# A streaming encoder layer on one core: the second pair of row tiles in both half-steps by eight products in place of seven

## The chip, the cores and the metric

The program runs on one core of a Trainium2 chip. The metric is the device time of one execution in microseconds (us). The kernel before takes 1363.33 us, the median of 3 runs (1361.89 to 1364.53).

## What is computed

One layer of an encoder for 592 tokens: 16 meta tokens, 512 of a prompt and 64 of a running stream, with model width 1024. It has five parts in a row, with residual adds:

```python
x = x + 0.5 * swiglu(rmsnorm(x, g1), ffn1_w1, ffn1_w3, ffn1_w2)
p = rmsnorm(x, g2) @ w_in
x = x + concat(rwkv(p), mla(p)) @ w_out
x = x + 0.5 * swiglu(rmsnorm(x, g3), ffn2_w1, ffn2_w3, ffn2_w2)
y = rmsnorm(x, g4)

def swiglu(h, w1, w3, w2):
    return (silu(h @ w1) * (h @ w3)) @ w2
```

The first and the fourth part are the two half-steps that the change touches. Their inner width is 2816, that is 22 row tiles of 128. The middle holds a recurrent mixer (8 heads, chunks of 64 tokens) and an attention (8 heads). Inputs and outputs are f32.

## The kernel before

**Number format.** A wide product is made of split operands: each weight and each activation is a high part, cast by ScalarE (ACT), and a low part, which is the remainder and is made by a subtraction (line 130) on VectorE (DVE) or GpSimd (POOL). One f32 product is then three matmuls, high by high, high by low, low by high (lines 153 to 155 in `mm3`, 323 to 325 in `product`).

**A half-step** (`ffn`, tag f1 or f2). Tokens are cut into two halves of 296 columns (288 in f2). The row tiles go in 11 pairs, row tile p with row tile p + 11, and each row tile stands for a tile of w1 (j = 0) and one of w3 (j = 1). For one j, a pair is a two-by-two block product: two row tiles by two halves of the 1024 inputs (index kh), times two halves of the inputs by two halves of the tokens. It can be done in two ways:

- `plain`: eight block products, 24 matmuls of one token half for each output tile, 192 for a pair. The operands are the four plain blocks "11", "21", "12", "22" (the input x times its gain, split). The norm's factor is applied when an output tile leaves PSUM (line 357, `scaled`), so the matmuls need no finished norm.
- `pair`: seven block products, 168 matmuls for a pair. It needs sums of weight blocks (lines 405 to 408, POOL, 1024 wide), their split parts, and four combined operand blocks "t1" to "t4", which need the norm of both token halves.

Pair 0 is done by `plain`, pairs 1 to 10 by `pair`. After them come the second products (`down`, outputs f1o and f2o, added into x at line 441); the first `down` needs pairs 0 and 1, and stands behind pair 2 in the program.

**Operands.** `Operands` makes the plain blocks (lines 258 and 259), the norm (squares added at line 169, line 176 sums, line 179 the reciprocal, line 183 spreads it) and, in `combined`, the blocks t1 to t4 in four steps: four products of x with gain and norm (line 277, DVE), four differences (line 279), four splits. ON_POOL says which of these go to POOL: in f1 the fourth difference and the splits of t1, t2 and t3, in f2 the split of t3. For pair 1 it also sends low parts of weight sums to POOL: s3 in f1, all four of s1 to s4 in f2.

**Order.** The string START[tag] interleaves the first steps: "a" and "b" step the operands of the two token halves, "t" the combined blocks, "0" and "1" the generators of pairs 0 and 1. The framework then places each instruction by a timeline of its own, on priorities that follow the order of writing. Each engine runs its queue strictly in the order that comes out; this holds for the middle of the program too. Weight blocks live in 7 buffers (raw2), their split parts in 4 + 4 (rings hi, lo, hi2, lo2), outputs in 8 PSUM banks. All transfers are issued from one queue, SP's.

In the middle, POOL solves 62 steps for each of 8 units of the mixer (lines 788 and 790). The result goes out to memory (line 792, qd), comes back (line 796, qt) and is transposed on DVE (line 803).

Of the kernel before, what the change touches and what calls it, by code (L numbers as in the profile page):

```python
# [45 lines left out]
ATTENTION = ((10, 0, 5), (11, 0, 4), (13, 0, 5), (13, 0, 7), (15, 0, 4), (12, 0, 7), (8, 0, 1), (11, 1, 13))  # L46


START = {"f1": "0aaaaaaa0aaa0babbbbbb0bbbb000tt00tt11", "f2": "aa0aaaaaba0ba1bb0babb0babb00b00tttt0"}
ON_POOL = {"n1": ("4", "t1", "t2", "t3"), "n1_0": ("sums",), "n1_1": (), "f1": ("s3",), "n2": ("t3",), "n2_0": (),  # L50
           "n2_1": (), "f2": ("s3", "s2", "s4", "s1")}
LOADS = ((0, (0,)), (0, (2,)), (0, (4,)), (0, (6,)), (0, ()), (1, (0, 2, 4, 6)))
AHEAD = 2
# [27 lines left out]
def build(ctx: ExitStack, tc: tile.TileContext, I, O):  # L81
# [64 lines left out]
    def mm3(outs, ws, xs, ks):  # L146

        n = len(ks)
        for out, w in zip(outs, ws):
            for i, k in enumerate(ks):  # L150
                xh, xl = xs(k)
                wh, wl = w[k]
                T.matmul(out, wh, xh, start=i == 0, stop=False)  # L153
                T.matmul(out, wh, xl, start=False, stop=False)  # L154
                T.matmul(out, wl, xh, start=False, stop=i == n - 1)  # L155
# [142 lines left out]
    def ffn(tag, x, ops, w13, w2, gp, n0, n1, between=iter(())):  # L298
# [9 lines left out]
        def parts(t, nm, sub=V):  # L308

            out = []  # L310
            for j, (pool, sfx) in enumerate(((ring, ""), (gp, "2"))):
                hi, lo = (pool.tile([128, 4, 128], F32R, tag=q + sfx, bufs=4, name=f"{nm}_{q[0]}{j}")
                          for q in ("hi", "lo"))
                split(hi, lo, t[:, j], sub)
                out.append((hi, lo))
            return out

        def product(nm, w, b):
            bh, bl = ops.get(b)
            for j, (wh, wl) in enumerate(w):  # L320
                out = fbank(f"{nm}{j}")[:, :n]
                for k in range(4):
                    T.matmul(out, wh[:, k], bh[k], start=k == 0, stop=False)  # L323
                    T.matmul(out, wh[:, k], bl[k], start=False, stop=False)
                    T.matmul(out, wl[:, k], bh[k], start=False, stop=k == 3)  # L325
                yield j, out

        def blocks(nm, p):
            A = {}
            for i, kh in ((0, 0), (0, 1), (1, 0), (1, 1)):  # L330
                A[i, kh] = gp.tile([128, 2, 4, 128], F32, tag="raw2", bufs=7, name=f"{nm}A{i}{kh}")
                src = w13[p + HM * i][:, :, 4 * kh:4 * kh + 4]
                if p == 0 and i == 0:
                    for j in range(2):
                        next(between, None)
                        nc.sync.dma_start(A[i, kh][:, j], src[:, j])
                else:
                    next(between, None)
                    nc.sync.dma_start(A[i, kh], src)
            return A  # L340

        def scratch(nm, tag, bufs=2):
            return [gp.tile([128, 296], F32, tag=tag, bufs=bufs, name=f"{nm}{j}")[:, :n] for j in range(2)]

        def gate(nm, p, i, h, h1, h3):
            si = tmp.tile([128, 320], F32, tag="sq", name=f"{nm}si{i}{h}")[:, :n]
            S.activation(si, h1, AF.Silu)
            if p == HM - 1 and (i, h) == (1, 0):
                load_sqrt(eps[:, 0:1])
            V.tensor_tensor(si, si, h3, ALU.mult)  # L350
            gh, gl = (gp.tile([128, 296], F32R, tag=q, bufs=12, name=f"{nm}{q}{i}{h}")[:, :n] for q in ("gh", "gl"))
            split(gh, gl, si)
            gs[2 * p + i, h] = gh, gl

        def scaled(t, ps, h):

            V.tensor_tensor(t, ps, ops.scale(h), ALU.mult)

        def plain(p):

            nm = f"{tag}_{p}"
            A, w = blocks(nm, p), {}
            yield
            for h in range(2):
                outs = {}
                for i in range(2):
                    if h == 0:
                        for kh in range(2):
                            for j, v in enumerate(parts(A[i, kh], f"{nm}w{i}{kh}")):
                                w[i, j, kh] = v  # L370
                    for j in range(2):
                        outs[i, j] = fbank(f"{nm}c{i}{h}{j}")[:, :n]
                        mm3([outs[i, j]], [{(kh, k): [t[:, k] for t in w[i, j, kh]] for kh in range(2) for k in range(4)}],
                            lambda k: [t[k[1]] for t in ops.get(f"{k[0] + 1}{h + 1}")],
                            [(kh, k) for kh in range(2) for k in range(4)])
                    yield
                for i in range(2):
                    c = scratch(f"{nm}c{i}{h}", ("p5", "u2")[i])
                    for j in range(2):
                        scaled(c[j], outs[i, j], h)  # L380
                    gate(nm, p, i, h, *c)
                    yield

        def pair(p):
            nm = f"{tag}_{p}"
            A = blocks(nm, p)
            s1 = gp.tile([128, 2, 4, 128], F32, tag="s1", bufs=1, name=f"{nm}s1")

            def sub(b):
                return G if p == 1 and b in ON_POOL[tag] else V  # L390

# [12 lines left out]
            yield
            G.tensor_tensor(s1, A[1, 0], A[1, 1], ALU.add)
            G.tensor_tensor(A[1, 0], A[0, 0], A[1, 0], ALU.subtract)
            G.tensor_tensor(A[0, 0], s1, A[0, 0], ALU.subtract)
            G.tensor_tensor(A[0, 1], A[0, 1], A[0, 0], ALU.subtract)
            yield
            u2, u3, p5 = sb("u2", "u2"), sb("u3", "u3"), sb("p5", "p5")  # L410
            for j, ps in product(nm + "p6", parts(A[0, 0], nm + "ws2", sub("s2")), "t2"):
                V.tensor_tensor(u2[j], ps, p1[j], ALU.add)
            for j, ps in product(nm + "p7", parts(A[1, 0], nm + "ws3", sub("s3")), "t3"):
                V.tensor_tensor(u3[j], ps, u2[j], ALU.add)
            for j, ps in product(nm + "p5", parts(s1, nm + "ws1", sub("s1")), "t1"):
                S.copy(p5[j], ps)
            for j in range(2):
                G.tensor_tensor(u2[j], u2[j], p5[j], ALU.add)
                G.tensor_tensor(p5[j], u3[j], p5[j], ALU.add)
            gate(nm, p, 1, 1, *p5)  # L420
            p3 = sb("p3", "p5")
            for j, ps in product(nm + "p3", parts(A[0, 1], nm + "ws4", sub("s4")), "22"):
                scaled(p3[j], ps, 1)
                G.tensor_tensor(u2[j], u2[j], p3[j], ALU.add)
            gate(nm, p, 0, 1, *u2)
            for j, ps in product(nm + "p4", parts(A[1, 1], nm + "w22"), "t4"):
                V.tensor_tensor(u3[j], ps, u3[j], ALU.add)
            gate(nm, p, 1, 0, *u3)
            yield

        def down(p0, np_, hs, *final):
            ks = range(2 * p0, 2 * p0 + 2 * np_)
            for m in range(KD):
# [160 lines left out]
    def project(i, names, also=(), pools=(None, None)):  # L594

        s, t = {}, {"r": 0, "k": 1, "v": 2}
        for nm in names:
            s[nm] = rp.tile([128, NRT], F32, tag="s", bufs=5, name=f"s{nm}_{i}")
            G.memset(s[nm][:, :PAD], 0.0)
        what = "lead" if also else "p"  # L600
        shift([j for j, _, _ in also] + [4 * t[nm] + i for nm in names], [nm for _, nm, _ in also] + [f"{nm}{i}" for nm in names],
              [d for _, _, d in also] + list(s.values()), ["wa"] * len(also) + [what] * len(names), pools)
        return s
# [23 lines left out]
    with tc.tile_pool(name="w0", bufs=4, side="right") as w0:  # L627
        first = project(0, "kr", ((12, "wa", swa), (13, "gl", sga)), (None, None, w0, w0))
# [694 lines left out]
```

## Time and profile before

| | us |
|---|---|
| median of 3 runs | 1363.33 |
| lowest and highest | 1361.89, 1364.53 |
| the profiled execution's own time | 1356.01 |
| its span, first to last instruction | 1354.2 |
| TensorE (PE) busy in the span | 1263.8 |
| VectorE (DVE) busy | 1063.9 |
| GpSimd (POOL) busy | 667.2 |
| ScalarE (ACT) busy | 624.2 |

The program has four stretches. f1 runs from 0 to about 420 us, the mixing from there to about 905 us, f2 to about 1340 us, the last norm and the stores to the end. A busy PE is not PE at its peak: its matmul records overlap (one lasts 0.30 us, the next begins 0.13 to 0.14 us later), and the granted clock says at what share of full speed it ran. A busy DVE can be an instruction that waits for a port; its length shows that beside the same form elsewhere.

### The profile page before, as it was taken

How to read it: one execution, taken by the hardware profiler on the slowest of the kernel's cores; microseconds unless marked ns; L12 is line 12 of the kernel's file. 1: busy time of each engine (PE TensorE's matmuls, PEld its weight loads, DVE VectorE, ACT ScalarE, POOL GpSimd, SP SyncE). 2: the span in 40 equal slices, each digit the busy share in tenths (PEclk: the TensorE clock that was granted, in tenths of full speed). 3: DMA queues.
4: the chain of work that ended last, by engine and by line, in shares of the span. 5: the costliest groups of instructions: out<-in, count | busy, mean ns of one | idle time of the engine just before them, and what ended most of it. 6: DMA issues, size and time to landing. Idle time of an engine off the chain costs nothing.

```text
span 1354.2 us, 26808 instructions
## 1 busy us (share of the span) xinstructions
PE 1263.8 (93%) x9984; PEld 1171.3 (86%) x9984; DVE 1063.9 (79%) x2073; ACT 624.2 (46%) x1389; POOL 667.2 (49%) x901
## 2 busy tenths in 40 slices
PE   7789999999999999999999689989689999999997
PEld 6789999999999988877776467879689999999997
DVE  7998888989876654667678465678998989898965
ACT  7443434334345554554565445456244434343443
POOL 3674546455477106464554552002763746464574
PEclk9899999999999998989999899999889999999998
DMA  8113232323115532212113112142123232323034
GB/s 277 47 49 92 94 94 77 104 70 100 42 36 169 169 91 63 68 47 59 46 52 106 31 38 54 34 156 85 47 78 83 75 99 89 94 94 95 17 86 140
DMA packets 88865, 113.32 MB, mean 84 GB/s; under 512 B 24672, under 2 KB 47392, under 8 KB 88736
## 3 DMA queue, kind: packets, MB, share of 16 engines
q1 hardware_dynamic: 88736, 111.62, 26.9%
q8 instruction: 79, 1.29, 0.4%
q14 instruction: 50, 0.41, 0.1%
HBM read 103.07 MB, written 8.52 MB: 82 GB/s over the span
## 4 chain that ended last, share of the span: by engine, by line
PE 71%; DVE 13%; DMA 4%; POOL 4%; issue 3%; ACT 3%; SPq 1%; DVEq 0%; POOLq 0%; ACTq 0%
PE f2o L153 3%; PE f2o L155 3%; PE f2o L154 3%; PE f1o L153 3%; PE f1o L154 3%; PE f1o L155 3%; DVE n L277 2%; POOL qm L790 1%; POOL tt L788 1%; DVE n L279 1%; PE f_10p L325 1%; PE f_4p L325 1%; PE f_8p L325 1%; PE f_6p L325 1%; PE f_8p L323 1%
## 5 line engine op out<-in xcount | busy, mean ns | idle before, releaser
L788 POOL TENSOR_TENSOR tt<-qm,up 80x60 f32<-80x60 f32 (+24 forms) x248 | 85.3, 344 | 63.0 <-DMA up<-ud 25.9
L790 POOL TENSOR_TENSOR qm<-qm,tt 80x60 f32<-80x60 f32 (+24 forms) x248 | 82.4, 332 | 18.4
L1067 POOL MEMSET P<- 128x112 f32 (+1 forms) x36 | 6.8, 191 | 124.5 <-PE ptp L1091 87.5
L441 DVE SCALAR_TENSOR_TENSOR x<-f1o,x 128x296 f32<-128x296 f32 x88 | 39.8, 460 | 24.8 <-PE f1o L155 24.7
L441 DVE SCALAR_TENSOR_TENSOR x<-f2o,x 128x288 f32<-128x288 f32 x88 | 38.7, 452 | 22.4 <-PE f2o L155 22.2
L153 PE MATMUL wo<-o,wo_h 128*128 128x288 f32 x128 | 43.4, 339 | 5.6 <-DVE x L975 4.6
L129 ACT CAST f1w_h<-f1w_r 128x512 fp32r<-128x512 f32 (+1 forms) x64 | 35.2, 563 | 26.0 <-PE f1o L154 18.7
L129 ACT CAST f2w_h<-f2w_r 128x512 fp32r<-128x512 f32 (+1 forms) x64 | 34.8, 562 | 25.7 <-PE f2o L154 18.9
L130 POOL TENSOR_TENSOR f1w_l<-f1w_r,f1w_h 128x512 fp32r<-128x512 f32 (+1 forms) x32 | 34.6, 1095 | 13.8 <-ACT f1w_h L129 11.6
L130 POOL TENSOR_TENSOR f2w_l<-f2w_r,f2w_h 128x512 fp32r<-128x512 f32 (+1 forms) x32 | 33.8, 1073 | 13.0 <-ACT f2w_h L129 10.2
L154 PE MATMUL wo<-o,wo_h 128*128 128x288 f32 x128 | 39.6, 309 | 0.0
L155 PE MATMUL wo<-o,wo_l 128*128 128x288 f32 x128 | 38.4, 300 | 0.0
L153 PEld LDWEIGHTS wo<-o,wo_h 128*128 128x128 f32 x128 | 24.2, 189 | 10.8 <-DVE x L975 6.4
L277 DVE SCALAR_TENSOR_TENSOR n<-x,vec,n_rs 128x296 f32<-128x296 f32 (+1 forms) x32 | 32.3, 1027 | 0.3
L674 POOL MEMSET e<- 128x5 f32 x8 | 0.9, 113 | 59.0 <-DVE bk L723 59.0
L1075 ACT ACTIVATE P<-s,m 128x264 f32<-128x264 f32 (+3 forms) x40 | 19.2, 482 | 22.7 <-DVE m L1073 19.3
L975 DVE TENSOR_TENSOR x<-wo,x 128x288 f32<-128x288 f32 x48 | 21.7, 452 | 9.3 <-PE wo L155 8.8
L153 PE MATMUL f_0c<-n_ops,f_0w_h 128*128 128x288 f32 (+1 forms) x96 | 28.5, 300 | 0.0
L154 PE MATMUL f_0c<-n_ops,f_0w_h 128*128 128x288 f32 (+1 forms) x96 | 28.2, 296 | 0.0
L155 PE MATMUL f_0c<-n_ops,f_0w_l 128*128 128x288 f32 (+1 forms) x96 | 28.2, 297 | 0.0
L1112 PE MATMUL s<-keys,qh 128*128 128x264 f32 (+3 forms) x80 | 27.0, 433 | 0.7 <-ACT pt L1097 0.5
L323 PE MATMUL f_1p<-n_ops,f_1ws_h 128*128 128x296 f32 (+1 forms) x48 | 16.1, 383 | 12.3 <-ACT n_ops L129 6.9
(1280 smaller groups left out, 5791.3 us busy)
## 6 DMA issues: line engine op xcount, KB each, us to landing
f1w_r<-in_w2a SPq DMA_DIRECT2D x48, 256.0 KB
f2w_r<-in_w2b SPq DMA_DIRECT2D x48, 256.0 KB
wo_r<-in_w_out SPq DMA_DIRECT2D x12, 256.0 KB
up<-ud SPq DMA_DIRECT2D x32, 80.0 KB
x<-in_xT SPq DMA_DIRECT2D x8, 296.0 KB
xd<-x SPq DMA_DIRECT2D x2, 1184.0 KB
x<-xd SPq DMA_DIRECT2D x2, 1152.0 KB
f_1A<-in_w13a SPq DMA_DIRECT2D x4, 512.0 KB
```

What stands on the lines that cost most here:

```text
L129: S.copy(dst_hi, src)
L130: sub.tensor_tensor(dst_lo, src, dst_hi.bitcast(F32), ALU.subtract)
L153: T.matmul(out, wh, xh, start=i == 0, stop=False)
L154: T.matmul(out, wh, xl, start=False, stop=False)
L155: T.matmul(out, wl, xh, start=False, stop=i == n - 1)
L277: V.scalar_tensor_tensor(b, x[h][:, kk], vcol(gain, kk), self.rs[h], ALU.mult, ALU.mult)
L323: T.matmul(out, wh[:, k], bh[k], start=k == 0, stop=False)
L325: T.matmul(out, wl[:, k], bh[k], start=False, stop=k == 3)
L441: V.scalar_tensor_tensor(x[h][:, m], o[:, :n], 0.5, x[h][:, m], ALU.mult, ALU.add)
L788: G.tensor_tensor(t3, qm[:, :nj, st:st + 1].to_broadcast([4 * NP, nj, w]), up[:, st:st + 1, st + 1:].to_broadcast([4 * NP, nj, w]), ALU.mult)
L790: G.tensor_tensor(qm[:, :nj, st + 1:], qm[:, :nj, st + 1:], t3, ALU.subtract)
L1112: T.matmul(s[:, :an], Q[:, hh, q0:q0 + 128], K[:, hh, a0:a0 + an], start=True, stop=True)
```

## The change

`plain` takes the order of the token halves as an argument. Pair 1 becomes a plain pair with the second token half first; `pair` is used from pair 2 on. The two strings of the first steps are written anew: all of pair 0, then the start of pair 1, and the four combined steps between its later ones.

```diff
-START = {"f1": "0aaaaaaa0aaa0babbbbbb0bbbb000tt00tt11", "f2": "aa0aaaaaba0ba1bb0babb0babb00b00tttt0"}
+START = {"f1": "0aaaaaaa0aaa0babbbbbb0bbbb00011001t1t1t11t11", "f2": "aa0aaaaaba0ba1bb0babb0babb00b00101t1t1t11t11"}
...
-        def plain(p):
+        def plain(p, hs):
...
-            for h in range(2):
+            for h in hs:
                 outs = {}
                 for i in range(2):
-                    if h == 0:
+                    if h == hs[0]:
...
-        first = [plain(0)] + [pair(p) for p in range(1, AHEAD)]
+        first = [plain(0, (0, 1)), plain(1, (1, 0))]
```

`pair` sends low parts to POOL for pair 1 alone (`p == 1`), so after the change no low part of a weight sum is made there; ON_POOL still holds for the operands. Lines behind the edit move by one or two (line 405 of before is line 406).

DVE in f1, from the reciprocal of the second half's norm on (n_12, n_22: combined operands; f_1w, f_1ws: low parts of weights of pair 1 and of its weight sums; f_0c: outputs of pair 0), before:

```order
L179 RECIPROCAL n_1_r<-n_1_r 128x3
L130 TENSOR_TENSOR f_1w_l_625<-f_1A_573,f_1w_h_624 128x512
L130 TENSOR_TENSOR f_1w_l_621<-f_1A_573,f_1w_h_620 128x512
L130 TENSOR_TENSOR f_1ws_l_680<-f_1A_571,f_1ws_h_679 128x512
L277 SCALAR_TENSOR_TENSOR n_12_0_471<-x_82,vec,n_rs_90 128x296
L277 SCALAR_TENSOR_TENSOR n_22_0_472<-x_82,vec,n_rs_90 128x296
L277 SCALAR_TENSOR_TENSOR n_12_1_491<-x_82,vec,n_rs_90 128x296
L277 SCALAR_TENSOR_TENSOR n_22_1_492<-x_82,vec,n_rs_90 128x296
```

The same place in the change:

```order
L179 RECIPROCAL n_1_r<-n_1_r 128x3
L130 TENSOR_TENSOR f_1w_l_489<-f_1A_470,f_1w_h_488 128x512
L130 TENSOR_TENSOR f_1w_l_485<-f_1A_470,f_1w_h_484 128x512
L130 TENSOR_TENSOR f_1w_l_569<-f_1A_472,f_1w_h_568 128x512
L357 TENSOR_TENSOR f_0c_553<-f_0c_418,n_rs_90 128x296
L277 SCALAR_TENSOR_TENSOR n_12_0_633<-x_82,vec,n_rs_90 128x296
L277 SCALAR_TENSOR_TENSOR n_22_0_634<-x_82,vec,n_rs_90 128x296
L277 SCALAR_TENSOR_TENSOR n_12_1_664<-x_82,vec,n_rs_90 128x296
L277 SCALAR_TENSOR_TENSOR n_22_1_665<-x_82,vec,n_rs_90 128x296
```

Plain weights of pair 1 (f_1w) stand where its weight sums (f_1ws) stood.

POOL in f1, behind the adds of the first half's norm (f_1s, f_1A, f_2s, f_2A: weight sums of pairs 1 and 2; n_ops, n_xh: splits of the combined operands), before:

```order
L405 TENSOR_TENSOR f_1s_579<-f_1A_575,f_1A_577 128x1024
L406 TENSOR_TENSOR f_1A_575<-f_1A_571,f_1A_575 128x1024
L407 TENSOR_TENSOR f_1A_571<-f_1s_579,f_1A_571 128x1024
L408 TENSOR_TENSOR f_1A_573<-f_1A_573,f_1A_571 128x1024
L130 TENSOR_TENSOR f_1ws_l_712<-f_1A_575,f_1ws_h_711 128x512
L130 TENSOR_TENSOR n_xh<-n_11_0_469,n_ops 128x296
L130 TENSOR_TENSOR f_1ws_l_716<-f_1A_575,f_1ws_h_715 128x512
L130 TENSOR_TENSOR n_ops<-n_12_0_471,n_ops 128x296
```

The same place in the change:

```order
L406 TENSOR_TENSOR f_2s_863<-f_2A_859,f_2A_861 128x1024
L407 TENSOR_TENSOR f_2A_859<-f_2A_855,f_2A_859 128x1024
L130 TENSOR_TENSOR n_ops<-n_12_0_633,n_ops 128x296
L279 TENSOR_TENSOR n_21_0_632<-n_21_0_632,n_22_0_634 128x296
L130 TENSOR_TENSOR n_xh<-n_22_0_634,n_xh 128x296
L130 TENSOR_TENSOR n_xh<-n_11_0_631,n_ops 128x296
L130 TENSOR_TENSOR n_xh<-n_11_1_662,n_ops 128x296
```

The four sums of pair 1 and its two low parts are gone, and two sums of pair 2 have come to the front of the queue.

SP's queue in the mixing, around the result of the solve of unit 2_1 (od: stores of mixed tokens; qd, qt: the solve's result out and back; ud, up: the next unit's data), before:

```order
L943 DMA od_5412<-ot_5_384_9166 128x128
L943 DMA od_5412<-ot_5_512_9198 128x64
L943 DMA od_5412<-xn_1_1_9078 128x320
L792 DMA qd_2_1_9816<-qm_2_1_9721 80x8x32
L796 DMA qt1_5436<-qd_2_1_9816 32x5x32 x2
L731 DMA ud_3_0_9378<-am_3_0_9358 32x5x32 x4
L796 DMA qt1_5436<-qd_2_1_9816 32x5x32 x2
L735 DMA up_3_0_9383<-ud_3_0_9378 20x1024 x4
```

The same place in the change:

```order
L794 DMA qd_2_1_9787<-qm_2_1_9692 80x8x32
L798 DMA qt1_5407<-qd_2_1_9787 32x5x32 x4
L785 DMA qm_3_0_10565<-in_rows 80x256
L945 DMA od_5383<-ot_5_384_9137 128x128
L945 DMA od_5383<-ot_5_512_9169 128x64
L945 DMA od_5383<-xn_1_1_9049 128x320
L1056 DMA wq3_0_10219<-in_wq 128x256
L733 DMA ud_3_0_9349<-am_3_0_9329 32x5x32 x4
```

Nothing of the mixing was edited; the placing came out another way from the middle of the attention on. Here the result's way out and back has moved ahead of three stores, and its four return loads now stand together.

## Rows read from the trace of the kernel before

**Rows 1.** The page: busy time of each engine over the span, then PE's busy tenths and its granted clock in 40 slices.

```profile
PE 1263.8 (93%) x9984; PEld 1171.3 (86%) x9984; DVE 1063.9 (79%) x2073; ACT 624.2 (46%) x1389; POOL 667.2 (49%) x901
...
PE   7789999999999999999999689989689999999997
...
PEclk9899999999999998989999899999889999999998
```

**Rows 2.** Busy time by stretches: the stretch, its length, busy time and instructions of PE, PEld, DVE, ACT and POOL, then granted clock, DMA share and GB/s. The first two run from the second half's reciprocal to the first low part for `down` in f1 and f2, the next two from PE's first matmul of pair 1 to the first of `down` in f1 and f2, the last two are later stretches of f1 and f2.

```profile
35.40:107.95 72.55, 57.09 (x355) 54.12 (x354) 70.96 (x92) 29.46 (x62) 49.85 (x36) 0.88 0.17 56
940.14:1015.36 75.22, 60.29 (x395) 58.15 (x394) 73.33 (x100) 29.32 (x61) 47.97 (x30) 0.86 0.17 56
40.86:111.11 70.25, 54.79 (x338) 52.00 (x337) 68.99 (x91) 27.57 (x58) 48.00 (x37) 0.88 0.20 64
952.52:1020.30 67.78, 52.85 (x338) 50.71 (x337) 67.71 (x93) 26.16 (x56) 45.54 (x31) 0.85 0.21 66
120.00:400.00 280.00, 280.00 (x2055) 280.00 (x2054) 241.60 (x357) 111.43 (x219) 151.79 (x98) 1.00 0.25 77
1030.00:1250.00 220.00, 220.00 (x1667) 220.00 (x1667) 196.04 (x292) 87.47 (x174) 118.35 (x73) 1.00 0.30 92
```

**Rows 3.** PE's waits in the two stretches of pairs 1 and 2, f1 then f2: who waited for whom, us in total, times, longest.

```profile
PE f_1p L323 <- DVE f_1c L357: 5.4, 1, 5.4
PE f_1p L323 <- ACT n_ops L129: 4.1, 2, 2.5
...
PE f_1p L323 <- ACT n_xh L129: 6.1, 2, 5.8
PE f_2p L323 <- DVE f_2p L357: 2.9, 2, 2.5
```

**Rows 4.** Timeline of DVE: start, length of the piece, instruction and how many; the first three and the fifth from places without a POOL instruction of two inputs beside them, the fourth (input in PSUM) with POOL work beside it, the last two from f2 beside the POOL rows of the next group.

```profile
906.57 0.69 DVE L130 TENSOR_TENSOR f_0w_l<-f_0A,f_0w_h 128x512 fp32r<-128x512 f32 x1 [1.30 <-ACT f_0w_h L129]
...
907.54 0.51 DVE L259 SCALAR_TENSOR_TENSOR n_ops<-x,vec,n_ops 128x288 fp32r<-128x288 f32 x1
...
121.23 0.83 DVE L441 SCALAR_TENSOR_TENSOR x<-f1o,x 128x296 f32<-128x296 f32 x2
45.17 0.82 DVE L357 TENSOR_TENSOR f_0c<-f_0c,n_rs 128x296 f32<-128x296 f32 x2
1002.61 1.28 DVE L130 TENSOR_TENSOR f_2ws_l<-f_2s,f_2ws_h 128x512 fp32r<-128x512 f32 x2
...
924.35 3.13 DVE L169 TENSOR_TENSOR n_acc<-n_acc,n_sq 128x288 f32<-128x288 f32 x2
927.40 2.63 DVE L259 SCALAR_TENSOR_TENSOR n_ops<-x,vec,n_ops 128x288 fp32r<-128x288 f32 x1
```

**Rows 5.** Timeline of POOL at that place.

```profile
924.78 2.37 POOL L405 TENSOR_TENSOR f_1s<-f_1A,f_1A 128x1024 f32<-128x1024 f32 x1 [37.86 <-DVE n_acc L169]
927.24 2.48 POOL L406 TENSOR_TENSOR f_1A<-f_1A,f_1A 128x1024 f32<-128x1024 f32 x1
```

**Rows 6.** POOL's groups that belong to pair 1, in f1 between 35.40 and 107.95 us: line, operation, tile and shape, how many, busy us and mean ns of one, idle time before them.

```profile
L130 POOL TENSOR_TENSOR f_1ws_l<-f_1A,f_1ws_h 128x512 fp32r<-128x512 f32 x2 | 3.1, 1530 | 0.0
L408 POOL TENSOR_TENSOR f_1A<-f_1A,f_1A 128x1024 f32<-128x1024 f32 x1 | 2.7, 2727 | 1.3 <-issue 1.3
L407 POOL TENSOR_TENSOR f_1A<-f_1s,f_1A 128x1024 f32<-128x1024 f32 x1 | 2.5, 2533 | 6.4 <-DVE f_1w_l L130 6.4
L418 POOL TENSOR_TENSOR f_1u<-f_1u,f_1p 128x296 f32<-128x296 f32 x2 | 2.5, 1236 | 1.2 <-DVE f_1u L414 1.2
L424 POOL TENSOR_TENSOR f_1u<-f_1u,f_1p 128x296 f32<-128x296 f32 x2 | 2.5, 1233 | 2.0 <-DVE f_1p L357 2.0
L419 POOL TENSOR_TENSOR f_1p<-f_1u,f_1p 128x296 f32<-128x296 f32 x2 | 2.2, 1096 | 0.1
L402 POOL TENSOR_TENSOR f_1c<-f_1c,f_1p 128x296 f32<-128x296 f32 x2 | 1.8, 930 | 0.8 <-ACT f_0gh L129 0.8
```

**Rows 7.** The same in f2 between 940.14 and 1015.36 us, the groups that differ in number from f1's.

```profile
L130 POOL TENSOR_TENSOR f_1ws_l<-f_1A,f_1ws_h 128x512 fp32r<-128x512 f32 x6 | 8.7, 1458 | 3.6 <-ACT f_1ws_h L129 3.6
L130 POOL TENSOR_TENSOR f_1ws_l<-f_1s,f_1ws_h 128x512 fp32r<-128x512 f32 x2 | 2.8, 1382 | 1.4 <-ACT f_1ws_h L129 1.4
```

**Rows 8.** SP's timeline in f1 (the pieces that load blocks of pair 2) and POOL's first sum of pair 2.

```profile
22.49 23.36 SPq L339 DMA_DIRECT2D f_2A<-in_w13a  x2
...
54.10 2.53 POOL L405 TENSOR_TENSOR f_2s<-f_2A,f_2A 128x1024 f32<-128x1024 f32 x1 [0.63 <-DVE f_1ws_l L130]
```

**Rows 9.** The solve of unit 2_1 in the mixing: PE's matmul behind its longest wait, DVE's wait between 740 and 775 us, and SP's timeline.

```profile
763.24 1.33 PE L854 MATMUL mps<-bkt,w 64*64 64x64 f32 x20 [9.64 <-ACT P L1075]
...
DVE q L803 <- DMA qt<-qd: 8.8, 1, 8.8
...
738.48 3.11 SPq L943 DMA_DIRECT2D od<-ot  x2
...
752.32 0.33 SPq L792 DMA_DIRECT2D qd<-qm  x1
755.86 0.81 SPq L796 DMA_DIRECT2D qt<-qd  x2
756.76 1.82 SPq L731 DMA_DIRECT2D ud<-am  x4
758.67 0.86 SPq L796 DMA_DIRECT2D qt<-qd  x2
```

## The prediction

> **What bounds the kernel now.** I read the page first. TensorE (PE) is busy 93% of the span, and its slices show where the rest is: of the 40 slices of 33.9 us the 2nd and 3rd (34 to 102 us) read 7 and 8, and those from 948 to 1016 us 6 and 8, with the digit of the granted clock at 8 in three of the four; most others read 9 and 9 [rows 1]. These are the pairs 1 and 2 of f1 and of f2. The windows give them numbers [rows 2]: from PE's first matmul of pair 1 to the first of `down` pass 70.25 us in f1 and 67.78 in f2, with PE busy 54.79 and 52.85 and a clock of 0.88 and 0.85. 336 matmuls run there (7 products of 24 for each of two pairs; the rows record two more). In later stretches at full clock a matmul takes 280/2055 = 0.1363 us (296 columns) and 220/1667 = 0.1320 us (288 columns), so 336 of them need 45.8 and 44.4 us. 24.5 and 23.4 us are lost to holes, and to the lower clock behind them.
>
> PE's waits say for whom [rows 3]: outputs that DVE had yet to take from PSUM (L357), and operands n_ops, n_xh whose source DVE makes (L277, L279). So I read DVE's own window, from the reciprocal of the second norm to the first low part for `down`: 72.55 us in f1 with DVE busy 70.96, 75.22 in f2 with 73.33 [rows 2]. DVE has no idle time there: its list sets the end of the stretch. And the list runs stretched. An instruction takes 0.60 us for a 512-wide low part, 0.435 for a product with a scalar vector, 0.37 to 0.40 for another of 296 columns [rows 4]; from a start to the next it is up to 0.1 less than the length shown, as the records overlap. By the order the window has in f1 24, 14 and 52 of these and a reciprocal: 24 x 0.60 + 14 x 0.435 + 52 x 0.373 = 40.0 us with the last. It took 70.96. What stretches it is POOL: a DVE add of 0.37 us and a product of 0.435 lasted 3.13 (two of them) and 2.63 us beside POOL's two 1024-wide sums of 2.37 and 2.48 us [rows 4, 5]. Not each instruction is held: the scaling of an output that sits in PSUM kept its 0.41 us with POOL at work [rows 4]. Over the window DVE's excess is 31.0 us while POOL is busy 49.85, that is **0.62 us lost for each us of POOL**; in f2 (19, 16, 63 and 1: 42.0) it is 31.4 over 47.97, or 0.65.
>
> The Trainium skill has a rule for that, in "SBUF — State Buffer", section "🔬 SBUF: two separate sides": VectorE and GpSimd share a port pair under an exclusive lock, and the loser blocks for the whole instruction. The rows above agree for single instructions, the windows only to two thirds. By 0.62 and 0.65 the sum below comes to 29.3 us, by a full lock it would be that of rival A.
>
> **The change part by part.**
>
> *Matmuls.* Pair 1 takes 192 in place of 168, 24 more in each half-step: 24 x 0.1363 = 3.3 and 24 x 0.1320 = 3.2 us. They lie where PE has holes of 15.5 and 14.9 us (length less busy). They cost something only if PE becomes the bound: 360 matmuls need 49.1 us in f1 and 47.5 in f2, so the stretches can shrink by 70.25 - 49.1 = 21.2 and 67.78 - 47.5 = 20.3 us at most. That floor caps every gain below: 41.5 us.
>
> *DVE's list.* By the order f1's list falls from 91 instructions to 84 (four low parts and five adds or evictions fewer, two products more): 20, 16 and 47 and the reciprocal, 36.6 us. f2's grows by three, since the low parts of weights that POOL made come to DVE as plain ones: 21, 16, 64 and 1, 43.5 us. So DVE's bare work falls 3.4 us in f1 and grows 1.5 in f2.
>
> *POOL's list.* In f1 go the rows of pair 1 [rows 6]: 3.1 for two low parts of sums, 2.7 and 2.5 for the two sums that lie in this window, 2.5 + 2.5 + 2.2 + 1.8 for the combinations: 17.4 us (17.3 by the rows, rounded). 49.85 - 17.4 = 32.5 us stay. In f2 go 8.7 + 2.8 of low parts [rows 7], sums of 2.4 + 2.5 (like those of rows 5), and combinations 2.5 + 2.5 + 2.2 + 1.9 (as in rows 6): 25.5 us; 22.5 stay.
>
> *The sum by DVE's list.* f1: 36.6 + 0.62 x 32.5 = 56.8, with the idle 1.6 of before 58.4, against 72.55: **-14.2**. f2: 43.5 + 0.65 x 22.5 = 58.2, with 1.9 idle 60.1, against 75.22: **-15.1**. Both stay under the cap, so DVE, not PE, still ends the stretch: PE's first `down` at 111.11 - 14.2 = 96.9, and in f2 at 1020.30 - 15.1 = 1005.2, less f1's shift 991.
>
> *Moved work.* POOL's sums of pair 2 come to the front of its queue in f1 (the order of the change). Before, the buffers of f_2A were held by pair 1's sums: SP stood at the f_2A loads from 22.49 for 23.36 us, and POOL's first f_2s began at 54.10 [rows 8]. Plain weights are free once they are split, so these loads end earlier and the 2.53 us sums run some 15 us earlier, at about 38 to 40, beside DVE work that they stretch as before. No term, as POOL's busy time is counted whole. Its neighbours behind it are the splits n_ops and n_xh, which PE needs only after 192 matmuls of pair 1, 26 us on. DVE's L277 products now stand behind plain weights and one eviction; PE asks for t1 later by those same 26 us. Plain outputs of pair 1 hold their PSUM banks until DVE scales them, as pair 0's do; if DVE came late, PE would wait as it does now [rows 3], and the sum by DVE's list has that in it.
>
> *The middle.* Nothing was edited, yet the order differs. The nearest row for its price is the solve of unit 2_1: PE waited 9.64 us at 753.6, DVE 8.8 for qt, because qd was issued at 752.32 and its return loads stood two before and two behind four ud loads, 755.86 to 758.67 [rows 9]. Together they would come 758.67 - 756.76 = 1.9 us sooner. Ends: a gain of 1.9 for each such place, or a loss of one such hole, 9.64. I take 0, since the same work of PE (its count is unchanged there) fills most of it, and keep both ends for the range.
>
> **Sum:** 14.2 + 15.1 = 29.3 us off. The profiled execution took 1356.01, which gives 1326.7; the median lies 7.3 above that, so 1363.33 - 29.3 = **1334**.
>
> **The rivals.**
>
> *A, the full relief.* Each us taken off POOL comes back to DVE whole, as the two rows of 3.13 and 2.63 us tell it [rows 4, 5]. f1: 17.4 + 3.4 = 20.8; f2: 25.5 - 1.5 = 24, capped by PE at 20.3. Together -41.1: 1322. For it: single rows are held for the length of POOL's. Against: 0.62 and 0.65 over the windows. The lock that the Trainium skill states (same page and section), taken strictly, gives this time.
>
> *B, no relief.* DVE's mean instruction stays at 70.96/91 = 0.78 and 73.33/99 = 0.741 us, because what remains on POOL comes to collide more densely (the sums of pair 2 move to DVE's busiest place). f1: 84 x 0.78 + 1.6 = 67.1, -5.4; f2: 102 x 0.741 + 1.9 = 77.5, +2.3. Together -3.1: 1360. Against: at the rows of the two later stretches, with POOL busy 151.79 of 280, DVE takes 241.60/357 = 0.68 [rows 2], so less POOL does mean shorter instructions.
>
> *C, the middle takes some back.* One more hole like that of unit 2_1, 9.64 us, or half of one: 1339 to 1344. It speaks for it that about 300 us of order changed, against it that the first half's gain is kept whatever the middle does.
>
> *D, slower.* In the changed queue of SP, qd stands ahead of three stores that were issued at 738.48, while it was issued at 752.32 [rows 9]. If SP waits at qd for the solve, all behind it, the od stores and the next unit's ud loads, waits those 13.8 us. If three units' solves put that on the path, it costs 41 us, more than the 29.3 gained: 1375. It decides from 29.3/13.8 = 2.1 units on. Against: stores have no reader for a long time, and the ud loads stood behind qd before too.
>
> **How the numbers follow.** Forecast 0.53 (both stretches shorten by DVE's list), A 0.20, B 0.12, C 0.11, D 0.04. The predicted time is the forecast's, 1334. Its own bounds are about 8 us to each side: an excess rate of 0.5 or 0.75 in place of 0.62 and 0.65 moves the sum by 6 to 7 us, a place in the middle by 2 to 10. The range takes in A's 1322 with the 1.9 us that the middle may give at two places, and C's end with the rate's bound, 1352: 1318 to 1352, which leaves out B and D, 0.16. About 0.2%, 2.7 us, is what a measurement of this kernel can tell. Faster: forecast, A and C, and most of B, 0.92; within: the rest of B, 0.04; slower: D, 0.04.
>
> **What would show it.** PE's first `down` at about 97 us in f1 (90 says A, 106 says B), and about 991 in f2. A granted clock near full from 50 to 90 us, and PE busy over 0.9 there. No f_1ws and no L402 of f_1 on POOL, whose busy time in the f1 window falls to about 32 us. DVE's mean instruction in f1's window near 0.68 us, in f2's near 0.57, with DVE still without idle time: if it idles, PE or ACT has become the bound. The sum of f1 alone is seen at the end of f1: its last `down` should stand 14 us earlier. For the middle, the time from the end of f1 to the start of f2 against that of before: a difference over 3 us is C or D, and PE's wait behind unit 2_1's solve tells at which place. The forecast is wrong if DVE's instructions stay at 0.78 us with less POOL work, or if PE waits at a plain output's bank for longer than now.

## The result, and the profile after

The changed kernel takes **1326.58 us**, the median of 4 runs (1322.19 to 1331.46), against 1362.61 before (1358.49 to 1364.53): a ratio of 0.974, 95% interval 0.9699 to 0.9782. The forecast was 1334. Run once more beside the other experiments it took 1326.26 against 1355.84, ratio 0.9767 (0.9739 to 0.9795). The profiled execution has a span of 1324.0 us (1354.2 before): 30.2 us less, where the sum said 29.3.

The page of the changed kernel: busy time, then PE's busy tenths and its granted clock by slices, to be read beside [rows 1].

```profile
PE 1263.4 (95%) x10032; PEld 1172.8 (89%) x10032; DVE 1029.8 (78%) x2063; ACT 615.9 (47%) x1373; POOL 615.5 (46%) x867
...
PE   7989999999999999999998889999999999999996
...
PEclk9989999999999989989998899999999999999998
```

PE has 48 matmuls more and the same busy time, POOL 52 us less to do. The dark slices of f2 are gone, those of f1 nearly so.

Its windows, to be read beside [rows 2] (length, busy time of PE, PEld, DVE, ACT, POOL, then clock): the first two from the second half's reciprocal to the first low part for `down`, the next two from PE's first matmul of pair 1 to the first of `down`.

```profile
32.85:95.99 63.14, 57.04 (x394) 56.20 (x392) 58.55 (x85) 25.75 (x55) 33.56 (x24) 0.92 0.18 59
924.13:987.07 62.94, 59.87 (x440) 59.40 (x439) 59.88 (x103) 27.66 (x58) 22.98 (x12) 0.97 0.18 59
40.24:99.27 59.03, 52.93 (x363) 52.09 (x362) 55.67 (x83) 24.40 (x54) 31.67 (x25) 0.91 0.18 57
937.35:990.20 52.85, 49.78 (x362) 49.30 (x361) 51.71 (x83) 22.29 (x49) 24.16 (x14) 0.97 0.18 58
```

POOL is busy 33.56 and 22.98 us, as forecast (32.5 and 22.5). DVE's windows fell from 72.55 to 63.14 and from 75.22 to 62.94, PE's stretches from 70.25 to 59.03 and from 67.78 to 52.85.

PE's waits in f1 (30 to 100 us) and, below the dots, in f2 (920 to 1000 us), to be read beside [rows 3].

```profile
PE f_2p L323 <- ACT n_xh L129: 3.3, 1, 3.3
PE f_2p L324 <- POOL n_xh L130: 2.2, 1, 2.2
PE f_2p L325 <- DVE f_2ws_l L130: 0.6, 1, 0.6
...
PE f_2p L324 <- POOL n_ops L130: 1.9, 1, 1.9
PE f_2p L323 <- ACT n_ops L129: 1.2, 1, 1.2
```

None stands in pair 1. What is left, 6.1 and 3.1 us, is pair 2's wait, all but 0.6 us of it for combined operands. Those holes keep f1 below full speed: from 50 to 90 us PE is busy 33.90 of 40 us at a clock of 0.87 (28.95 at 0.79 before), so the sign that the prediction named for this place, over 0.9 and near full, did not come.

All kernels side by side, from the starts of PE's first and last matmul of each output. "f1" and "f2" are the stretches from pair 1 to the first `down`; "middle" is from the last matmul of f1's `down` to f2's first of pair 1.

| kernel | f1 | first `down` of f1 at | middle | f2 | span | median, its before |
|---|---|---|---|---|---|---|
| before | 70.2 | 111.1 | 509.1 | 67.8 | 1354.2 | |
| before, second trace | 69.9 | 111.7 | 507.7 | 67.5 | 1353.8 | |
| changed | 59.0 | 99.3 | 505.2 | 52.9 | 1324.0 | 1326.58, 1362.61 |
| changed, second trace | 59.1 | 100.6 | 502.9 | 52.9 | 1324.5 | 1326.26, 1355.84 |
| f1 alone | 59.3 | 99.2 | 506.0 | 66.1 | 1337.4 | 1343.39, 1359.24 |
| f2 alone | 71.7 | 113.3 | 508.0 | 52.9 | 1341.1 | 1341.59, 1359.24 |
| POOL adds put back | 65.2 | 105.3 | 509.4 | 63.6 | 1345.6 | 1347.61, 1359.24 |
| POOL memsets put back | 55.9 | 95.7 | 504.8 | 58.1 | 1332.8 | 1334.63, 1355.84 |
| seven products, no POOL work | 60.2 | 100.1 | 527.0 | 49.5 | 1342.6 | 1344.82, 1359.24 |
| f1's splits on DVE | 56.8 | 97.3 | 503.9 | 52.9 | 1321.8 | 1322.43, 1357.87 |
| all splits on DVE | 56.8 | 96.7 | 505.3 | 54.5 | 1323.6 | 1322.63, 1355.84 |
| old order of first steps | 55.1 | 98.9 | 502.7 | 52.3 | 1322.1 | 1321.22, 1357.87 |
| halves 0, 1 | 61.1 | 101.6 | 523.2 | 56.0 | 1347.4 | 1349.14, 1357.87 |
| three plain pairs | 56.9 | 97.0 | 519.0 | 54.5 | 1337.5 | 1338.68, 1357.87 |

Where a half-step was not touched, its stretch came out at 69.9 to 71.7 (f1) and 66.1 to 67.8 us (f2): differences of under 2 us in one trace mean nothing. The middle came again within 2.3 us. One of the six runs of "POOL adds put back" was slow, 1721.12 us, and is not in its ratio; the median of the other five is 1347.44.

### The profile page after: what moved, and what is told of

Read it like the earlier page. It is cut to its first block, busy times and chain, and to the rows that moved or that the text cites. A ratio compares the mean times of both kernels' runs of the same rounds, so it can differ in the third digit from the quotient of the medians.

```text
span 1324.0 us, 26812 instructions
## 1 busy us (share of the span) xinstructions
PE 1263.4 (95%) x10032; PEld 1172.8 (89%) x10032; DVE 1029.8 (78%) x2063; ACT 615.9 (47%) x1373; POOL 615.5 (46%) x867
## 4 chain that ended last, share of the span: by engine, by line
PE 74%; DVE 8%; DMA 6%; POOL 5%; issue 3%; ACT 3%; SPq 1%; DVEq 0%; POOLq 0%; ACTq 0%
PE f2o L155 3%; PE f2o L153 3%; PE f2o L154 3%; PE f1o L155 3%; PE f1o L153 3%; PE f1o L154 3%; POOL qm L792 2%; POOL tt L790 2%; PE wo L153 1%; PE f_8p L325 1%; PE f_4p L325 1%; PE f_10p L325 1%; PE f_6p L325 1%; PE f_5p L325 1%; PE f_6p L323 1%
## 5 line engine op out<-in xcount | busy, mean ns | idle before, releaser
L790 POOL TENSOR_TENSOR tt<-qm,up 80x60 f32<-80x60 f32 (+24 forms) x248 | 81.2, 327 | 62.2 <-DMA up<-ud 31.2
L792 POOL TENSOR_TENSOR qm<-qm,tt 80x60 f32<-80x60 f32 (+24 forms) x248 | 87.1, 351 | 18.4
L129 ACT CAST f1w_h<-f1w_r 128x512 fp32r<-128x512 f32 (+1 forms) x64 | 35.0, 562 | 26.4 <-PE f1o L154 17.1
L129 ACT CAST f2w_h<-f2w_r 128x512 fp32r<-128x512 f32 (+1 forms) x64 | 34.8, 563 | 25.4 <-PE f2o L154 11.3
L406 POOL TENSOR_TENSOR f_2s<-f_2A,f_2A 128x1024 f32<-128x1024 f32 x2 | 5.1, 2569 | 83.3 <-DVE n L279 64.6
L977 DVE TENSOR_TENSOR x<-wo,x 128x288 f32<-128x288 f32 x48 | 21.5, 452 | 11.3 <-PE wo L155 11.1
L155 PE MATMUL f_1c<-n_ops,f_1w_l 128*128 128x288 f32 (+1 forms) x96 | 28.4, 296 | 0.0
L154 PE MATMUL f_1c<-n_ops,f_1w_h 128*128 128x288 f32 (+1 forms) x96 | 28.4, 296 | 0.0
L153 PE MATMUL f_1c<-n_ops,f_1w_h 128*128 128x288 f32 (+1 forms) x96 | 28.4, 296 | 0.0
```

Source lines behind the costliest of these rows:

```text
L129: S.copy(dst_hi, src)
L790: G.tensor_tensor(t3, qm[:, :nj, st:st + 1].to_broadcast([4 * NP, nj, w]), up[:, st:st + 1, st + 1:].to_broadcast([4 * NP, nj, w]), ALU.mult)
L792: G.tensor_tensor(qm[:, :nj, st + 1:], qm[:, :nj, st + 1:], t3, ALU.subtract)
L977: V.tensor_tensor(x2s[h][:, m], ps[:, :n], x2s[h][:, m], ALU.add)
```

## The experiments

**Each half-step alone.**

```diff
+        first = [plain(0, (0, 1)), plain(1, (1, 0)) if tag == "f1" else pair(1)]
```

(and "f2" in the second kernel; START of the other half-step as before)

> Only f1 gets the change; f2 is as before. If each half-step gains by its own stretch: first `down` of f1 at about 99 us as in the changed kernel (111.1 before), the stretch of pairs 1 and 2 in f2 at 67.8 us as before, and the whole 12 us shorter than before, or up to 16 shorter if the middle's 3.4 us of the changed kernel come from its new order. Rival (the middle's order eats or makes the gain): the time from the end of f1 to the start of f2's pair 1 moves by more than 5 us, either way.

> Only f2 gets the change; f1 is as before. By the stretches: first `down` of f1 at 111.1 us, the stretch of pair 1 and 2 in f2 at about 53 us (67.8 before), the whole 15 us shorter, or up to 18 with the middle's 3.4 us. Rival: a middle that moves by more than 5 us.

Measured: ratios 0.9896 (0.9868 to 0.9925) and 0.9874 (0.985 to 0.9898). Each half-step shrank by itself as in the changed kernel, and the other stayed. The spans fell by 16.8 and 13.1 us, together 29.9, the changed kernel's 30.2; the medians fell by 15.9 and 17.7. The middle moved by 3 us with f1's change and by 1 with f2's, so it neither made nor ate the gain.

**The POOL work put back.** `plain` for p = 1 gets adds that nobody reads.

```diff
+    if p == 1:
+        for r in range({"f1": 2, "f2": 4}[tag]):
+            u, v = (w[i, j, kh][0].rearrange("p a b -> p (a b)")[:, :n].bitcast(F32) for j in range(2))
+            G.tensor_tensor(extra, u, v, ALU.add)
...
+    if p == 1:
+        for j in range(2):
+            G.tensor_tensor(extra, c[0], c[1], ALU.add)
```

> The changed kernel with about as much POOL work put back as it took away: 16 adds of 296 columns in f1 and 24 of 288 in f2, two inputs in SBUF, whose result nobody reads; the output is unchanged. Theory (POOL's work stretches DVE's list, 0.65 to 0.71 us per us): 16 x 1.05 x 0.65 = 11 us back in f1's window, 24 x 1.05 x 0.71 = 18 in f2's, first `down` of f1 at about 110, the whole 25 to 29 us above the changed kernel. Rival (what gains is that PE has 192 matmuls to run which need no combined operand, and the POOL work was not in the way): under 5 us above the changed kernel.

Measured: ratio 0.9925 (0.9898 to 0.9952); of the 30.2 us of span 21.6 went, 4.2 of them in the middle. Windows of DVE's list in f1 and f2, as above:

```profile
32.63:102.06 69.43, 57.27 (x394) 55.73 (x393) 65.75 (x84) 25.36 (x54) 49.26 (x39) 0.93 0.17 54
934.53:1008.24 73.71, 63.40 (x442) 61.30 (x441) 71.28 (x102) 27.31 (x58) 46.40 (x36) 0.93 0.15 51
```

DVE does the same instructions and is busy 7.2 and 11.4 us longer, for 15.7 and 23.4 us of POOL. The stretches grew by 6.2 and 10.8. That is well over the rival's 5 us, but the rate is 0.46 and 0.49, not 0.65 to 0.71. In f2, where ACT and PE have the order of the changed kernel and DVE's differs in three steps, PE waits mostly for parts that DVE makes, and the sum of pair 2 that POOL has there waits for DVE too:

```profile
PE f_2p L325 <- DVE f_2w_l L130: 2.8, 3, 1.7
PE f_2p L325 <- DVE f_2ws_l L130: 2.7, 1, 2.7
PE f_2p L324 <- DVE n_xh L130: 2.1, 1, 2.1
...
976.97 2.55 POOL L417 TENSOR_TENSOR f_2A<-f_2s,f_2A 128x1024 f32<-128x1024 f32 x1 [4.53 <-DVE f_2w_l L130]
```

**The same POOL time, without reads.** Each of these adds is replaced by:

```diff
-            G.tensor_tensor(extra, u, v, ALU.add)
+            G.tensor_tensor(extra[:, :1], u[:, :1], v[:, :1], ALU.add)
+            for _ in range(3):
+                G.memset(extra, 0.0)
```

> The kernel with the POOL work put back, but each added add (two inputs of 296 columns) is replaced by an add of one column, which holds it at its place, and three memsets of 296 columns, which read nothing; the output is unchanged. Theory (POOL's work costs by its port: reads of SBUF by both engines): the added POOL time of about 15 to 25 us in each half-step costs DVE nearly nothing, stretches within 2 us of the changed kernel. Rival (it costs by standing in POOL's queue ahead of the sums and splits that PE needs): f1's stretch 6 and f2's 11 us longer than in the changed kernel, as the adds made them.

Measured: ratio 0.9835 (0.9805 to 0.9865). The windows again, f1 and f2:

```profile
32.41:94.40 61.99, 55.77 (x384) 55.05 (x383) 55.79 (x82) 24.89 (x53) 51.47 (x81) 0.94 0.18 60
925.16:986.58 61.42, 53.76 (x391) 52.71 (x389) 56.19 (x94) 26.17 (x55) 46.38 (x88) 0.96 0.19 61
```

POOL is as busy as with the adds (51.47 and 46.38), but DVE's busy time is 55.79 and 56.19 us for 82 and 94 instructions, a mean of 0.68 and 0.60 (changed kernel: 58.55 for 85 and 59.88 for 103, 0.69 and 0.58; with the adds 65.75 for 84 and 71.28 for 102, 0.78 and 0.70). So POOL's time alone doesn't stretch DVE. The end of the stretch is another matter. The table's "f1" and "f2" of this kernel end early, as its last 24 matmuls of pair 2 stand behind the first `down`; 3.3 and 3.2 us must be added to compare: 59.2 in f1 (59.0 in the changed kernel), 61.3 in f2, 8.4 us longer. In f1 the theory held; in f2 the time came near the rival's 11. POOL's timeline there shows the queue: memsets before and between the two sums of pair 2 that PE waits for.

```profile
960.93 1.11 POOL L377 TENSOR_TENSOR f_1extra<-f_1w_h,f_1w_h 128x1 f32<-128x1 f32 x1
962.10 0.74 POOL L379 MEMSET f_1extra<- 128x288 f32 x2
962.80 2.42 POOL L421 TENSOR_TENSOR f_2A<-f_2s,f_2A 128x1024 f32<-128x1024 f32 x1
965.13 0.36 POOL L379 MEMSET f_1extra<- 128x288 f32 x1
965.43 2.42 POOL L422 TENSOR_TENSOR f_2A<-f_2A,f_2A 128x1024 f32<-128x1024 f32 x1
```

PE's waits in f2, and below the dots the DVE row that ends the first of them:

```profile
PE f_2p L323 <- DVE f_1c L357: 5.1, 1, 5.1
PE f_2p L323 <- ACT f_2ws_h L129: 3.9, 1, 3.9
...
987.79 0.81 DVE L357 TENSOR_TENSOR f_1c<-f_1c,n_rs 128x288 f32<-128x288 f32 x2
```

The second is the cast of these sums, which end at 967.85 against 963.99 in the changed kernel; pair 1 began 1.0 us later here, so they are 2.8 us late. That is the rival's queue. The first is not: DVE's order came out another way in f2, and pair 1's last two scalings stand at 987.79, where the changed kernel's last is at 968.48. So the memsets' 8.4 us in f2 mix the queue with another order of DVE, and say little of the 10.8 us that the adds cost there. With the adds PE had no wait for a cast of the sums, and DVE's list was longer by itself; what share of the 10.8 the adds' place in the queue has stays open. In f1 it is the port: the same POOL time without reads cost 0.2 us, with them 6.2.

**Seven products without POOL's part.** The kernel before; for p = 1 the four sums and the adds on POOL are left out, and for the parts that `sub` gave to POOL the high part stands for the low part.

```diff
-                return G if p == 1 and b in ON_POOL[tag] else V
+                return None if p == 1 and b in ON_POOL[tag] else V
...
+            if p == 1:
+                s1 = A[1, 1]
+            else:
                 G.tensor_tensor(s1, A[1, 0], A[1, 1], ALU.add)
...
+                if p > 1:
                     G.tensor_tensor(u2[j], u2[j], p5[j], ALU.add)
```

> The kernel before with pair 1 still by seven products, but without its POOL work: the weight sums, the low parts that POOL made and the adds of the combinations are left out (the plain block or the high part stands in their place), so the output is not that of the layer. Theory (POOL stretches DVE's list): f1's first `down` about 12 us earlier, f2's stretch about 16 shorter, the whole 25 to 28 us below before. Rival (PE needs the plain products as cover while the combined operands are made): PE's waits for n_ops and n_xh in pair 1 stay, and the whole gains 10 us at most.

Measured: ratio 0.9902 (0.988 to 0.9923), only 14 us. But both stretches fell as the theory said: f1's first `down` 11.0 us earlier, f2 18.3 us shorter, with no plain product in pair 1. DVE's windows, f1 and f2, to be read beside [rows 2]:

```profile
32.59:97.96 65.37, 56.13 (x378) 52.90 (x377) 62.65 (x90) 30.17 (x63) 34.96 (x24) 0.97 0.17 57
946.42:1007.59 61.17, 57.74 (x427) 56.29 (x426) 58.06 (x104) 31.08 (x66) 24.08 (x12) 1.00 0.19 61
```

DVE is busy 8.3 and 15.3 us less for 14.9 and 23.9 us less of POOL, 0.56 and 0.64 us for each, with about as many instructions as before. Of the rival's waits, those of pair 1 for n_ops and n_xh, f1 kept 5.5 of 5.8 us and f2 1.0 of 11.3; both stretches shrank all the same. So cover by plain products isn't needed for the gain. What the whole lost is in the middle, which took 527.0 us in place of 509.1.

**The combined operands' splits on DVE.**

```diff
-ON_POOL = {"n1": ("4", "t1", "t2", "t3"), ...
+ON_POOL = {"n1": (), ...
```

(in the second kernel "n2": () too)

> The changed kernel with the 16 small steps of f1's combined operands (fourth difference, low parts of t1, t2, t3) on DVE in place of POOL; f2 unchanged. Theory with the rate 0.65: DVE's bare list in f1's window grows by 16 x 0.373 = 6.0 us, POOL loses about 17 us, 11 us of excess go: DVE busy 53.5 in place of 58.6, first `down` of f1 some 4 us earlier. Rival (small POOL steps cost DVE only about 0.46 us per us, as the added ones did): 7.8 go for 6.0, under 2 us gained. Rival 2 (a step on POOL runs beside DVE for nothing): 6 us lost.

> The changed kernel with f1's 16 and f2's 4 small operand steps on DVE, none on POOL (the run with f1's 16 alone gave a stretch 2.3 us shorter in f1). Theory (a us off POOL frees 0.5 of DVE, a step costs DVE 0.37): f1's stretch 56.8 us, f2's 4 steps 4 x 0.97 x 0.5 = 2.0 freed for 1.5, and PE's 1.9 us wait for POOL's n_ops gone: about 51 to 52.5 us (52.9 now); the whole 2 to 4 us below the changed kernel. Rival (nothing left to gain: the stretch is held by the order of the operands): within 1 us.

Measured: f1's stretch 2.3 us shorter in both, between theory and rival: POOL lost 14.9 us in the window, DVE got 6.0 us of work and was busy 57.29 in place of 58.55, so 7.3 us of excess went, 0.49 for a us. Its idle time fell too, from 4.6 to 2.3 us. The window, with f1's splits on DVE:

```profile
33.17:92.72 59.55, 54.20 (x384) 53.48 (x383) 57.29 (x102) 26.66 (x56) 18.67 (x9) 0.97 0.19 63
```

In f2 the four steps gained nothing (54.5 against 52.9): PE now waits 3.9 us for n_xh on DVE. As a whole, 0.9738 (0.9703 to 0.9772) and 0.9742 (0.9713 to 0.977) against the changed kernel's 0.9767 (0.9739 to 0.9795): the intervals overlap. By stretches the first is 2.3 us ahead of the changed kernel.

**Order of the first steps, order of the halves, a third plain pair.** In these three the result isn't the layer's. The high parts of t1 and t4 lie in the place of block "12" (`"12": b[4:]`, then `"t1": (b[4], c[0]), "t4": (b[5], c[1])`), and here a plain pair reads half 1's block "12" after they overwrote it, so its products wait for the combined operands' casts (in the runs' traces PE f_1c waits for ACT n_ops L129). That is what the reversed halves are for: pair 1 must be done with half 1 before the combined steps begin.

```diff
-START = {"f1": "0aaaaaaa0aaa0babbbbbb0bbbb00011001t1t1t11t11", ...
+START = {"f1": "0aaaaaaa0aaa0babbbbbb0bbbb000tt00tt11", ...
```

> The changed kernel (pair 1 by eight products, halves reversed) with the two strings of the first steps as they were before: the four combined steps stand ahead of pair 1's products. Theory (the sum of DVE's list and POOL's work sets the end, not its order): f1's first `down` and f2's stretch within 3 us of the changed kernel, the holes lie in pair 1 rather than in pair 2. Rival (the new order of the steps is what gains, since it puts plain work in front): 8 to 20 us above the changed kernel.

```diff
-        first = [plain(0, (0, 1)), plain(1, (1, 0))]
+        first = [plain(0, (0, 1)), plain(1, (0, 1))]
```

> The changed kernel with pair 1's token halves in the order 0, 1. Theory: PE has no hole in pair 1, so the order of its halves costs and gains nothing: within 2 us. Rival (the reversed order is needed, because half 0's outputs and operands are not there when pair 1 begins): over 4 us above the changed kernel, with PE waits in pair 1.

```diff
-        first = [plain(0, (0, 1)), plain(1, (1, 0))]
+        first = [plain(0, (0, 1)), plain(1, (1, 0)), plain(2, (0, 1))]
```

> The changed kernel with pair 2 by eight products as well (token halves in the order 0, 1), its steps after and between those of pair 1; 24 matmuls more in each half-step. Theory (what is still lost, 10 us in f1 and 5 in f2, are holes and low clock behind operands and outputs that DVE and POOL make late for pair 2): they go, the stretch from pair 1 to the first `down` comes to its floor, 384 x 0.1363 = 52.3 us in f1 (59.0 now) and 384 x 0.1320 = 50.7 in f2 (52.9 now); the whole about 8 us below the changed kernel. Rival (the lists just move the holes to pair 3, and the extra matmuls are paid): 2 x 3.2 = 6.5 us above it.

Measured: the old order (0.9729, 0.97 to 0.9759) has its first `down` at 98.9 us (99.3 and 100.6 in the changed kernel) and f2 at 52.3. Its waits, 7.1 us for n_ops, lie in pair 1, as the theory said. The order isn't what gains. With halves 0, 1 (0.9931, 0.9905 to 0.9956) PE waits for n_ops in pair 1, and the stretches are only 2.1 and 3.2 us longer; the rest of its 23.4 us of span is 18 us more middle, which no theory had. Three plain pairs (0.9849, 0.9814 to 0.9884): f1 is 2.1 us shorter, f2 1.7 longer, PE waits 2.7 and 1.6 us for low parts f_2w_l. Neither bound came; the 24 extra matmuls eat what the holes give back, and the median's 12 us are the middle, 13.9 us longer.

**Both kernels once more.**

> The changed kernel once more, beside the others of this set: 33 us below before, f1's stretch 59.0 and f2's 52.9 within 1.5 us; the middle (last output of f1 to the first `wo` product) 364 to 366 us, if it hangs on the order of the queues and not on chance.

> The kernel before once more, for a second trace: f1's stretch 70 to 72 us, f2's 66 to 68, the middle 367.5 to 368.5 us with the same hole of 9 to 10 us in front of the solve's unit 2_1.

Measured as in the table: the stretches of f1 and f2 came again within 0.5 us. The rest missed by a little: the changed kernel is 29.6 us below its before and not 33, the wait at the solve of unit 2_1 was 7.6 us (9.64 in [rows 9]), and from f1's last `down` to the first `wo` product before took 368.4 and 367.3 us, changed 364.1 and 363.7.

## Why the prediction was right

**DVE's list, stretched by POOL, bounds the stretch: shown.** Taking POOL's work out of the old pair 1 gave 10.1 and 18.3 us by itself; putting reads back stretched nearly the same list by 7.2 and 11.4 us; putting writes back did not stretch its instructions. Rival B fell with that. Rival A fell too: DVE's excess over its bare list is 58.55 - 36.6 = 22.0 us for 33.56 of POOL in f1 and 16.4 for 22.98 in f2, 0.65 and 0.71, near the 0.62 and 0.65 of before and not 1. On the margin it is less: from before to changed 9.0 us of excess for 16.3 of POOL (0.56), and 15.0 for 25.0 (0.60). By its time A, 1322, lies nearer to the measured 1326.58 than the forecast; the stretches tell them apart, 11.8 us of gain in f1 and 14.9 in f2 where A asked 20.8 and 20.3.

**f2's term: mis-sized too, 15.1 for 12.3 in its own window.** DVE was busy 59.88 us, not 58.2, and idle 3.1, not 1.9. PE's stretch fell by 14.9 all the same: the first `down` came 3.1 us behind the window's end (4.9 before), and pair 1 began 0.8 us later behind the reciprocal. The prediction had no term for either, so that 14.9 lies so near 15.1 is luck in part.

**f1's term: mis-sized, 14.2 for 9.4, and a term missing beside it.** DVE was busy 58.55 us, not 56.8, and idle 4.6, not the 1.6 of before: small waits for ACT (the cast f_1w_h, the activations f_0si and f_1si) and for POOL's splits, whose buffers L277 needs. "The idle 1.6 of before" was a carry-over with no row for it. DVE's waits in f1's window of the changed kernel:

```profile
DVE f_1w_l L130 <- ACT f_1w_h L129: 1.1, 2, 0.7
DVE f_0si L350 <- ACT f_0si L347: 0.9, 1, 0.9
...
DVE n L277 <- POOL n_xh L130: 0.7, 1, 0.7
DVE n L277 <- POOL n_ops L130: 0.5, 1, 0.5
DVE f_1si L350 <- ACT f_1si L347: 0.5, 1, 0.5
```

The missing term: pair 1's first two sums ran at 23 to 28 us, ahead of my window, beside the second norm's adds. These rows of DVE, before and below it changed, show it.

```profile
22.47 6.72 DVE L169 TENSOR_TENSOR n_acc<-n_acc,n_sq 128x296 f32<-128x296 f32 x5
35.40 0.18 DVE L179 RECIPROCAL n_r<-n_r 128x3 f32<-128x3 f32 x1 [0.45 <-ACT n_r L178]
```

```profile
22.70 2.72 DVE L169 TENSOR_TENSOR n_acc<-n_acc,n_sq 128x296 f32<-128x296 f32 x5
...
32.85 0.18 DVE L179 RECIPROCAL n_r<-n_r 128x3 f32<-128x3 f32 x1 [0.88 <-ACT n_r L178]
```

Five adds took 4.0 us less, and the window began 2.55 us earlier. 9.4 + 2.55 makes, to 0.1, the 11.8 us (111.1 to 99.3) that f1 gained. "Seven products, no POOL work" and "POOL adds put back", which both lack these two sums, have that reciprocal at 32.59 and 32.63 us. In f2 the first two sums ran ahead of the window too [rows 4, 5]; with f2's change alone the reciprocal stands 494.0 us behind the end of f1 for 496.7 and 495.3 before, but pair 1's start hardly moved (508.0 for 509.1 and 507.7).

**The middle: 0 taken, about 4 us gained, and the loss priced too low.** The hole of 9.64 us was priced as a loss only; in the new order it is gone, and with the change of f1 the middle took 502.9 to 506.0 us in six of seven traces of that order (509.4 in the one with POOL's adds) for 507.7 to 509.1 in the old one. Rival C's place was right and its sign wrong. Its price was too small: "halves 0, 1" and "seven products, no POOL work" got another order of the untouched middle and paid 18 us, "three plain pairs" a third one and paid 13.9. The windows of the changed kernel and, below, of "halves 0, 1", both 330 to 430 us behind the end of f1, show where a part of it lies:

```profile
762.20:802.20 40.00, 36.13 (x412) 26.10 (x406) 24.54 (x79) 21.78 (x70) 27.16 (x88) 0.96 0.17 40
802.20:862.20 60.00, 57.40 (x545) 48.41 (x545) 34.00 (x105) 27.90 (x76) 7.21 (x26) 0.97 0.15 40
```

```profile
765.10:805.10 40.00, 36.11 (x352) 26.07 (x352) 22.54 (x72) 14.45 (x46) 22.53 (x78) 0.74 0.11 26
805.10:865.10 60.00, 52.74 (x468) 42.98 (x465) 26.59 (x84) 27.77 (x77) 9.69 (x34) 0.89 0.15 40
```

PE gets 137 fewer matmuls through, at a clock of 0.74 and 0.89 for 0.96 and 0.97. Which row of the order decides it stays open; no run changed the middle alone. Rival D (qd ahead of the stores) didn't happen: no wait of PE in the changed middle is over 2.0 us.

**The sum.** 11.8 (f1) + 3.9 (middle) + 14.9 (f2), less 0.4 elsewhere, is 30.2, for a forecast of 29.3. The mechanism was right, the closeness is luck: the two windows that the sum was made of gave 9.4 + 12.3 = 21.7 us, and what they lacked came from the sums ahead of f1's window, from PE's side of f2 and from the middle. The median came 7 us under the forecast because I carried over the 7.3 us between the profiled execution of before and its median; the changed kernel's median lay 0.8 us above its profiled execution, and in the later sets before's median was 1355.84 to 1359.24.

## What to carry to other kernels

Where a saturated DVE shares a stretch with POOL, count POOL's instructions that read SBUF as DVE work, at about half to two thirds of their time, and look for sums on POOL ahead of the window as well as in it. Doing 24 matmuls more on an engine that stands in holes can be the cheapest way to take that work out, until they cost as much as the holes give back (the third pair). If a scheduler places the whole program, price the untouched part on both sides: here it moved by -4 to +18 us, as much as either edit.

## What the runs showed of the hardware

An instruction of DVE is held as a whole or not at all. The 16 products of L277 in f1's window of the changed kernel, then of the kernel with the adds put back (duration in ns, least, median, most):

```profile
L277 DVE SCALAR_TENSOR_TENSOR n<-x,vec,n_rs x16: 511/524/2661, 36.6 to 80.7; 128x296 f32<-128x296 f32 x16
```

```profile
L277 DVE SCALAR_TENSOR_TENSOR n<-x,vec,n_rs x16: 510/1078/2657, 36.7 to 88.2; 128x296 f32<-128x296 f32 x16
```

The median is unstretched in the first. Nine of its 16 took 511 to 527 ns; the seven others each ended 0.32 to 0.33 us behind the end of the POOL instruction that they ran into. Here the longest, and the sum on POOL beside it, which ended at 68.07 us:

```profile
65.74 2.66 DVE L277 SCALAR_TENSOR_TENSOR n<-x,vec,n_rs 128x296 f32<-128x296 f32 x1
...
65.46 2.61 POOL L408 TENSOR_TENSOR f_2A<-f_2s,f_2A 128x1024 f32<-128x1024 f32 x1 [2.20 <-DVE f_2w_l L130]
```

Eight scalings of outputs in PSUM (L357) took 455 ns each on average in the same window, three of them wholly beside POOL's work. DVE's steps with two SBUF inputs that ran beside memsets of POOL alone (346 ns each) kept their length: a 512-wide low part at 958.50 us, for example, took 0.68 us.

```profile
L357 DVE TENSOR_TENSOR f_1c<-f_1c,n_rs 128x296 f32<-128x296 f32 x8 | 3.6, 455 | 0.0
```

```profile
L394 POOL MEMSET f_1extra<- 128x296 f32 x21 | 7.3, 346 | 0.7
```

The Trainium skill, "SBUF — State Buffer", section "🔬 SBUF: two separate sides", names for the lock, beside a mode of DVE that takes two ports, DVE instructions with two SBUF inputs, and those only against GpSimd instructions that read SBUF. These runs agree: reads cost 0.46 to 0.71 of POOL's time, writes nothing that shows (mean DVE instruction 0.68 and 0.60 us with the memsets, 0.69 and 0.58 without). The prediction took a full lock to mean rival A; the lock is full for each instruction here, and a stretch still loses less than POOL's time. Why is only argued: POOL's own time is stretched too (of the splits of 128 x 296 in the changed kernel one took 0.82 us at 50.77 and another 1.28 at 61.99), and part of it falls beside DVE instructions on PSUM, which it doesn't hold.
